# Linear attention's output gates as four pairs of half-size products

## The chip, the cores and the metric

One core of one Trainium2 chip. The metric is the device time of one execution in microseconds (us), the median of several. On the core, TensorE (PE) multiplies, ScalarE (ACT) and VectorE (DVE) do the elementwise work, GpSimd (POOL) and SyncE (SP) mostly start DMA transfers. Each works through its own list of instructions, and semaphores tie the lists together.

## The reference, cut to what matters

The program is a decoder of two layers over 528 tokens (16 of them meta tokens) with a width of 1024. Each layer has two feed-forward networks (FFNs) around a mixer. The mixer of the first layer is the gated linear attention (GLA) that the change is about:

```
q, k, v, r, lr = split(hn @ w_in)            # 512, 512, 1024, 1024, 16 columns
gk = log_sigmoid(lr @ w_gate + b_gate) / 16
... per head (4) and chunk (64): o = causal(q_dec k_dec^T) v + q_dec state
o = rmsnorm(o, g_head) * silu(r)             # r: the output gates
return o @ w_out
```

The gates are r = hn @ w_r, 1024 x 1024 over 528 tokens: eight tiles of 128 rows of r each.

## The kernel before, in words

Everything is computed in fp32 accuracy from pairs of an upper and a lower part: a value w becomes w0 = round(w) (an ACT copy to fp32r) and w1 = w - w0 (a DVE subtraction), and a product is the sum of three matmuls, w0 x0, w1 x0 and w0 x1. `mm3` and its relatives record them all at L202.

TensorE's order is written out by the Python code itself. Generators ("jobs") yield estimated times to a virtual clock (`Flow`, L76 on); whatever records matmuls advances the clock by their cost, and a job goes on when the clock has come to it. ACT's, DVE's and POOL's lists are then made from that recording by the scheduler, so the yields (STEP, STATE_KEYS 1.5, SCALED 2.2, BEHIND 2.2) decide how much other work stands between two steps of a job, not how long anything waits on the chip. Weights come in units. `load_unit` issues a unit's DMAs on SP into "raw" slots (13 of 128 x 512), `split_unit` makes the two parts of a plain unit (ACT L271, DVE L274), `set_ahead` says how far loading runs ahead. A unit that is a list of two tiles is made by `split_pair` into the seven factors 11, s1, s2, 12, s3, s4, 22 of a Strassen product (ACT L291, DVE L292): the sums s1 to s4 come partly from two accumulating DMAs on POOL (L350), partly from DVE additions (L297). All parts, of weights and of tokens alike, share one pool of 40 "pair" slots (128 x 2 x 528).

The FFNs' two large products run that way: `Strassen` holds the PSUM banks, an `Item` runs seven half-size products (two halves of the rows by two halves of the 528 tokens), and `right_factors` makes the seven token factors 11, t1, 22, t2, 21, t3, t4 (ACT L998, DVE L999, differences L1008) from scaled copies xs of the residual H (L1013). Since the factors need room, `right_factors` writes H to DRAM (`h_kept`), and later code brings it back.

GLA ran with plain tiles instead. In the stage (`gla`, from L1228) the first four tiles k, q, v, v of head 0 come first, then for each head h the coroutine `core(h)` runs while `x_units` multiplies the next head's four tiles. `core` holds the scans of the log gates (L1307, L1308), transposes of the values (pv), exponentials, keys' transposes (pk), scores (pa, pb), states (ps), outputs (po, pn), the reciprocal roots of the outputs' norms (`half_roots`, ten small DVE steps L477 to L486 on a tile half_go), the scaling of the outputs with them on ACT (on, L1406, and onm for the meta tokens, L1407), and transposes back (pt, PE L214). Behind head 3's tiles `x_units` multiplies the eight gate tiles, each over token groups of 272 and 256 columns, while heads 2's end and head 3 run. `gated(m, g, p)` takes one tile and group: times the token norm (L1430), tanh on ACT, the gate (L1432), times the head's output (L1437), then split into parts og (ACT L540, DVE L541). `out_proj` multiplies og by the output weights (y on PE).

## Time and profile before

| | us |
|---|---|
| median of three runs | 1844.48 (1844.38 to 1844.85) |
| the profiled execution itself | 1848.01 |
| its span, first to last instruction | 1846.2 |
| PE busy in the span | 1834.5 |
| DVE, ACT busy | 1459.9, 1119.6 |
| the GLA stage's heads and gates (405 to 557 us): DVE busy | 102.0 of 152 |
| the last 198 matmuls of the gate tiles | 533.0 to 557.2 |

How to read it: the span is that of one profiled execution, the median that of unprofiled ones; differences worked out in the span are carried over to the median. A row of a timeline is start, length, engine, line, operation, out<-in, shape, count, and in brackets how long the engine was idle before it and who ended that. Names in the profile leave out buffer numbers: x is a tile's PSUM bank, w a weight part, zl0f a token factor of layer 0's first FFN, w_s a weight sum, half_go the roots.

### The profile page before, as it was taken

To read this page: it belongs to the slowest core of one execution; us is meant where nothing else is said; L and a number is where in the kernel's file an instruction comes from. 1 tells how busy PE (TensorE), PEld (TensorE's weight loads), DVE (VectorE), ACT (ScalarE), POOL (GpSimd) and SP (SyncE) were. 2 spreads that over 40 slices of the span, in tenths; PEclk is the share of its full clock that TensorE was granted. 3 is DMA by queue.
4 is the path that set the end of the run, shared out by engine and by line. 5 is a ranking of instruction groups with operands and counts; after the bars stand their busy time and mean duration, and the time that the engine had idled before them with its cause. 6 is when DMAs were issued, how large, how long until landed. Compare 5 with 4: busy or idle time off the path is not lost.

```text
span 1846.2 us, 38789 instructions
## 1 busy us (share of the span) xinstructions
PE 1834.5 (99%) x14743; PEld 1780.8 (96%) x14743; DVE 1459.9 (79%) x3029; ACT 1119.6 (61%) x2613; POOL 324.0 (18%) x487
## 2 busy tenths in 40 slices
PE   9999999999999999999999999999999999999998
PEld 9999999999999999999999899999987898999998
DVE  6889888666664788988878789898667678898884
ACT  6666666654446566665665566666558765666564
POOL 2210101320001411011133110112320042111122
PEclk9999999999999999999999999999999999999999
DMA  6756659421213366666853565768421226657681
GB/s 244 196 152 156 166 150 247 151 70 58 69 58 115 105 173 154 155 167 151 252 180 104 143 161 148 181 151 243 153 80 47 70 91 162 161 152 175 156 252 49
DMA packets 143371, 269.98 MB, mean 146 GB/s; under 512 B 16080, under 2 KB 36432, under 8 KB 143184
## 3 DMA queue, kind: packets, MB, share of 16 engines
q1 hardware_dynamic: 113056, 194.94, 32.8%
q0 software_dynamic: 29696, 71.97, 19.6%
q8 instruction: 115, 1.88, 0.4%
q14 instruction: 72, 0.59, 0.1%
q10 hardware_dynamic: 432, 0.59, 0.1%
HBM read 230.74 MB, written 36.18 MB: 145 GB/s over the span
## 4 chain that ended last, share of the span: by engine, by line
PE 93%; DVE 4%; ACT 2%; issue 1%; DMA 1%; DVEq 0%; SPq 0%; POOLq 0%; ACTq 0%
PE a L202 28%; PE x L202 22%; PE y L202 17%; PE c L202 13%; PE d L202 7%; PE o L202 1%; DVE w L292 1%; PE po L202 1%; DVE w_s L292 1%; ACT s L1623 1%; DVE raw L297 1%; DMA raw<-in_w_in 1%; ACT w_s L291 0%; PE pt L214 0%; PE sa L202 0%
## 5 line engine op out<-in xcount | busy, mean ns | idle before, releaser
L292 DVE TENSOR_TENSOR w_s<-raw,w_s 128x512 fp32r<-128x512 f32 (+1 forms) x416 | 264.2, 646 | 73.6 <-ACT w_s L291 69.6
L291 ACT ACTIVATE w_s<-raw 128x512 fp32r<-128x512 f32 (+1 forms) x416 | 241.0, 592 | 89.2 <-DVE raw L324 49.2
L292 DVE TENSOR_TENSOR w<-raw,w 128x512 fp32r<-128x512 f32 (+1 forms) x312 | 196.2, 645 | 4.0
L274 DVE TENSOR_TENSOR w<-raw,w 128x512 fp32r<-128x512 f32 x248 | 164.5, 695 | 37.0 <-ACT w L271 34.7
L350 POOL DMA_DIRECT2D raw<-in_w_in x112 | 103.4, 967 | 453.2 <-DVE w L292 97.1
L291 ACT ACTIVATE w<-raw 128x512 fp32r<-128x512 f32 (+1 forms) x312 | 177.7, 589 | 0.0
L297 DVE TENSOR_TENSOR raw<-raw,raw 128x512 f32<-128x512 f32 (+1 forms) x256 | 162.7, 636 | 2.2
L202 PE MATMUL x<-x_l0m,w 128*128 128x272 f32 (+1 forms) x1152 | 152.2, 289 | 0.0
L202 PEld LDWEIGHTS x<-x_l0m,w 128*128 128x128 f32 x1152 | 143.4, 188 | 2.7 <-issue 1.7
L271 ACT ACTIVATE w<-raw 128x512 fp32r<-128x512 f32 x248 | 144.1, 620 | 2.5 <-DMA raw<-in_w_in 1.2
L535 POOL TENSOR_TENSOR acc_post<-acc_post,sq_post 128x256 f32<-128x256 f32 (+1 forms) x77 | 61.7, 802 | 360.8 <-ACT sq_post L534 357.2
L202 PE MATMUL y<-hidl0f,w 128*128 128x272 f32 (+1 forms) x960 | 119.3, 285 | 0.0
L202 PEld LDWEIGHTS y<-hidl0f,w 128*128 128x128 f32 x960 | 117.9, 188 | 0.2
L202 PE MATMUL a<-zl0f_t,w_s 128*128 128x264 f32 x864 | 116.8, 284 | 0.0
L202 PE MATMUL y<-hidl1f,w 128*128 128x256 f32 (+1 forms) x768 | 114.8, 310 | 0.0
L202 PE MATMUL a<-zl1f_t,w_s 128*128 128x256 f32 x864 | 113.8, 281 | 0.0
L202 PEld LDWEIGHTS y<-hidl1f,w 128*128 128x128 f32 x768 | 104.9, 188 | 8.5
L202 PEld LDWEIGHTS a<-zl0f_t,w_s 128*128 128x128 f32 x864 | 109.9, 188 | 0.0
L202 PEld LDWEIGHTS a<-zl1f_t,w_s 128*128 128x128 f32 x864 | 107.1, 188 | 0.0
L1213 POOL DMA_DIRECT2D kept_y<-dn x32 | 36.3, 1134 | 400.5 <-DVE w_s L292 203.7
L202 PE MATMUL x<-x_l0f,w 128*128 128x256 f32 (+1 forms) x768 | 98.9, 289 | 1.5 <-ACT w L271 1.1
L202 PEld LDWEIGHTS x<-x_l0f,w 128*128 128x128 f32 x768 | 96.2, 191 | 2.2 <-ACT w L271 1.3
(568 smaller groups left out, 4118.7 us busy)
## 6 DMA issues: line engine op xcount, KB each, us to landing
raw<-in_w_in SPq DMA_DIRECT2D x408, 256.0 KB, 4.2
raw<-in_w_in POOLq DMA_DIRECT2D x112, 256.0 KB, 5.4
raw<-in_w_down SPq DMA_DIRECT2D x128, 192.0 KB, 2.4
raw<-in_w_last SPq DMA_DIRECT2D x48, 256.0 KB, 4.9
raw<-in_gla_in SPq DMA_DIRECT2D x48, 256.0 KB, 3.2
kept_y<-dn POOLq DMA_DIRECT2D x16, 528.0 KB, 8.2
raw<-in_w_out SPq DMA_DIRECT2D x32, 256.0 KB, 3.1
kept_y<-dn POOLq DMA_DIRECT2D x16, 512.0 KB, 8.6
```

The source lines that it names most:

```text
L202: inst = pe.matmul(o, lhs, rhs, start=start, stop=stop, skip_group_check=onto)
L271: high = act.activation(w[:, 0, :m], raw[:, :m], AF.Copy)
L274: dve.tensor_tensor(w[:, 1, :m], raw[:, :m], w[:, 0, :m].bitcast(F32), op=ALU.subtract)
L291: act.activation(w[:, 0, :m], src, AF.Copy)
L292: dve.tensor_tensor(w[:, 1, :m], src, w[:, 0, :m].bitcast(F32), op=ALU.subtract)
L297: return dve.tensor_tensor(dst, dst, src, op=ALU.add)
L350: added = pool.dma_start(r, src, accum_op=ALU.add)
L535: pool.tensor_tensor(sums[0][:, :n], sums[0][:, :n], t[:, :n], op=ALU.add)
L1213: pool.dma_start(y_sum[:, 2 * self.q : 2 * self.q + 2, o : o + 2 * n], self.y[:, :, : 2 * n], accum_op=ALU.add)
L1623: act.activation(s[:, c], s[:, c], AF.Exp, scale=rc[:, c % 2 : c % 2 + 1], bias=nm[:, c : c + 1], accum_out=den[:, c : c + 1],)
```

## The change

The sixteen plain units of the heads stay; the eight gate tiles become four paired units 64 to 67 (`GLA_PAIRS`). When the code comes to head 1, a job makes the token factors (`right_factors` for GLA's own normed input, with its differences' and parts' pace at 1.2 instead of STEP 1.1). Three of its four scratch tiles come from another pool ("dn"), so H goes out to DRAM here too and its four loads back (`bring_back_h`) stand on POOL behind the gates. The first paired unit waits in `plain` until the first parts are made. A new `Projected` runs the seven products of a pair and puts the two tiles of gates together from them; one c bank instead of two. Gating then works on one tile of 528 columns at a time. Loading ahead is set to 16 with a ring instead of 8. The heads 1 to 3 yield BESIDE = 3.0 more before the keys' transposes and 1.5 more before the transposes back; head 0 has the room that it had.

```diff
-GLA_ORDER = [4, 0, 8, 9, 5, 1, 10, 11, 6, 2, 12, 13, 7, 3, 14, 15] + list(range(16, 24))
+GLA_ORDER = [4, 0, 8, 9, 5, 1, 10, 11, 6, 2, 12, 13, 7, 3, 14, 15]
+GLA_PAIRS = [(16, 17), (18, 19), (20, 21), (22, 23)]
...
+                units += [[a["gla_in"][u] for u in pair] for pair in GLA_PAIRS]
...
-        xs = [pair_tile(f"xs{x.name}_{k}", F32) for k in range(0, KD, 2)]
+        xs = [yp.tile([P, 2, TOK], F32, tag="dn", name=f"xs{x.name}_{k}") for k in range(0, KD - 2, 2)]
+        xs.append(pair_tile(f"xs{x.name}_{KD - 2}", F32))
...
+    class Projected(Item):
+        nk = 4
...
+        def body(self):
+            self.product(self.c, "s1", "t1", True)
+            act.activation(self.second[1], self.c, AF.Copy, scale=self.scale)
+            self.product(self.a, "s2", "t2", False)
+            act.activation(self.first[1], self.a, AF.Copy)
+            self.product(self.d, "12", "21", False)
+            act.activation(self.first[0], self.d, AF.Copy)
+            self.product(self.a, "s3", "t3", False)
+            dve.scalar_tensor_tensor(self.second[1], self.a, self.scale, self.second[1], op0=ALU.mult, op1=ALU.add)
+
+        def tail(self):
+            self.product(self.c, "s4", "22", False)
+            dve.tensor_tensor(self.first[1], self.c, self.first[1], op=ALU.add)
+            self.product(self.a, "22", "t4", False)
+            act.activation(self.second[0], self.a, AF.Copy, scale=self.scale)
...
-                yield STATE_KEYS + (0 if h else BEHIND)
+                yield STATE_KEYS + (BESIDE if h else BEHIND)
...
-                yield SCALED
+                yield SCALED + (BESIDE / 2 if h else 0)
...
-            def gated(m, g, p):
+            def gated(m):
+                gs, th = rg[m]
                 act.activation(th, gs, AF.Tanh, scale=0.5)
+                yield 0.8
                 dve.scalar_tensor_tensor(gs, th, 1.0, gs, op0=ALU.add, op1=ALU.mult)
+                yield cores[m // 2]
+                yield 0.8 + m % 2 * 1.5
...
+                if h == 1:
+                    flow.spawn(right_factors(x, halves, z, plain, 1.2))
...
-            set_ahead(8)
-            x_units(x, KD, L0, lambda i, g, p: jobs.append(flow.spawn(gated(i, g, p))))
-            flow.wait(*jobs[:12])
+            plain.finish(flow)
+            set_ahead(16, RING)
+            tiles = Strassen(z, halves, 1)
...
+            bring_back_h(slice(0, TOK))
+            flow.wait(*jobs[:6])
```

How instructions move is shown at three places; numbers in names are buffer numbers.

First, the last six of the ten reciprocal-root steps of head 2 on DVE (half_go2), before the change, with what followed them (V1_3 are value rows of head 3, b3 its scans):

```order
L481 TENSOR_SCALAR half_go2_6431<-half_go2_6431 128x5
L482 TENSOR_TENSOR half_go2_6431<-half_go2_6431 128x5
L483 SCALAR_TENSOR_TENSOR half_go2_6431<-half_go2_6431 128x5
L484 TENSOR_TENSOR half_go2_6431<-half_go2_6431 128x5
L485 SCALAR_TENSOR_TENSOR half_go2_6431<-half_go2_6431 128x5
L486 SCALAR_TENSOR_TENSOR half_go2_6431<-half_go2_6431 128x5
L1256 TENSOR_TENSOR V1_3_6479<-x63_0_6387,R_l0m_5018 128x272
L1256 TENSOR_TENSOR V1_3_6479<-x63_1_6388,R_l0m_5018 128x256
L274 TENSOR_TENSOR w67_0_6534<-raw67_0_6475,w67_0_6534 128x512
L274 TENSOR_TENSOR w67_1_6537<-raw67_512_6477,w67_1_6537 128x512
L1307 SCALAR_TENSOR_TENSOR b3_6570<-resets_4978,ls23_5498 128x528
L1308 SCALAR_TENSOR_TENSOR b3_6570<-resets_4978,ls23_5498 128x528
```

After the change DVE has there (zl0m_t30 is a token factor, w64 are factors of the first pair):

```order
L1293 TENSOR_TENSOR V1_3_6500<-x63_1_6389,R_l0m_5018 128x256
L480 TENSOR_SCALAR half_go2_6508<-sums2_6463 128x5
L295 TENSOR_TENSOR w64_11_6546<-raw64_0_6488,w64_11_6546 128x512
L481 TENSOR_SCALAR half_go2_6508<-half_go2_6508 128x5
L1006 SCALAR_TENSOR_TENSOR zl0m_t30_6596<-xsl0m_0_5735,zl0m_t30_6596 128x528
L482 TENSOR_TENSOR half_go2_6508<-half_go2_6508 128x5
L1344 SCALAR_TENSOR_TENSOR b3_6599<-resets_4978,ls23_5498 128x528
L483 TENSOR_TENSOR half_go2_6508<-half_go2_6508 128x5
L1345 SCALAR_TENSOR_TENSOR b3_6599<-resets_4978,ls23_5498 128x528
L484 TENSOR_SCALAR half_go2_6508<-half_go2_6508 128x5
L300 TENSOR_TENSOR raw64_0_6488<-raw64_0_6488,raw64_3_6491 128x512
L485 TENSOR_TENSOR half_go2_6508<-half_go2_6508 128x5
```

What stood behind the roots now stands between their steps, along with parts of the pair and of the tokens. ACT's list behind the scaling of head 2's outputs is, after the change:

```order
L1444 ACTIVATE onm2_6462<-pn2_6460,half_go2_6508 16x256
L1352 ACTIVATE vt3_6602<-pv3_0_6603 128x4x128
L1005 ACTIVATE zl0m_t31_6624<-xsl0m_2_5736 128x528
L294 ACTIVATE w65_11_6647<-raw65_0_6581 128x512
L1125 ACTIVATE d64_6577<-a64_0_6574 128x264
L1352 ACTIVATE vt3_6602<-pv3_1_6618 128x4x128
L1453 ACTIVATE V1_2_6074<-pt2_0_6628 128x512
L1005 ACTIVATE zl0m_t40_6650<-xsl0m_4_5737 128x528
L1453 ACTIVATE V1_2_6074<-pt2_1_6640 128x512
L1361 ACTIVATE d3_6653<-b3_6599 128x528
L1363 ACTIVATE d3_6653<-b3_6599 128x528
L294 ACTIVATE w64_s1_6660<-raw64_3_6491 128x512
```

The upper part of s1 of pair 64 has become the eleventh instruction behind onm2.

Second, PE's list between head 2's transposes back (pt2) and those of head 3's values (pv3), before the change (x64 is the last tile of head 3, x65 the first gate tile):

```order
L214 MATMUL pt2_1_6527<-ident_78,on2_6404 128x128 x4
L1415 MATMUL pm2_t_6513<-ident_78,onm2_6405 128x16
L202 MATMUL x64_0_6482<-x_l0m_5_4924,w63_1_6127 128x272 x3
L202 MATMUL x64_1_6483<-x_l0m_5_4924,w63_1_6127 128x256 x3
L202 MATMUL x64_0_6482<-x_l0m_6_4951,w63_1_6127 128x272 x3
L202 MATMUL x64_1_6483<-x_l0m_6_4951,w63_1_6127 128x256 x3
L202 MATMUL x64_0_6482<-x_l0m_7_5000,w63_1_6127 128x272 x3
L202 MATMUL x64_1_6483<-x_l0m_7_5000,w63_1_6127 128x256 x3
L202 MATMUL x65_0_6565<-x_l0m_0_4802,w64_0_6240 128x272 x3
L214 MATMUL pv3_0_6574<-ident_78,V1_3_6479 128x128 x4
L202 MATMUL x65_1_6566<-x_l0m_0_4802,w64_0_6240 128x256 x3
L202 MATMUL x65_0_6565<-x_l0m_1_4828,w64_0_6240 128x272 x3
```

and the same place after it, where 57 matmuls of the tiles x63 and x64 stand between pn2 and the first row:

```order
L204 MATMUL d64_6577<-zeros_81 128x264
L204 MATMUL a64_0_6574<-zl0m_110_5883,w64_11_6546 128x264 x3
L216 MATMUL pv3_0_6603<-ident_78,V1_3_6500 128x128 x4
L204 MATMUL a64_0_6574<-zl0m_110_5883,w64_11_6546 128x264 x3
L204 MATMUL a64_0_6574<-zl0m_111_5922,w64_11_6546 128x264 x6
L216 MATMUL pv3_1_6618<-ident_78,V1_3_6500 128x128 x4
L216 MATMUL pt2_0_6628<-ident_78,on2_6461 128x128 x4
L1452 MATMUL pm2_t_6627<-ident_78,onm2_6462 128x16
L216 MATMUL pm3_6636<-ident_78,V1_3_6500 16x128 x2
L216 MATMUL pt2_1_6640<-ident_78,on2_6461 128x128 x4
L1452 MATMUL pm2_t_6627<-ident_78,onm2_6462 128x16
L204 MATMUL c64_0_6576<-zl0m_t10_5994,w64_s1_6660 128x264 x6
```

All tiles of head 3 now stand ahead of pt2, and in place of the gate tile x65 stand the first two products of pair 64, one per factor.

Third, DVE's list ahead of the last two tiles of the gated output, og6 and og7, before the change:

```order
L1437 SCALAR_TENSOR_TENSOR rg7_7276<-rg7_7276,vec_77,V1_3_6479 128x272
L1437 SCALAR_TENSOR_TENSOR rg7_7276<-rg7_7276,vec_77,V1_3_6479 128x256
L541 TENSOR_TENSOR og7_7283<-rg7_7276,og7_7283 128x272
L274 TENSOR_TENSOR w75_0_7324<-raw75_0_7252,w75_0_7324 128x512
L541 TENSOR_TENSOR og7_7283<-rg7_7276,og7_7283 128x256
```

and after it (w72 to w75 are weights of the output projection):

```order
L1466 SCALAR_TENSOR_TENSOR rg6_7128<-rg6_7128 128x528
L1471 SCALAR_TENSOR_TENSOR rg6_7128<-rg6_7128,vec_77,V1_3_6500 128x528
L1466 SCALAR_TENSOR_TENSOR rg7_7129<-rg7_7129 128x528
L1471 SCALAR_TENSOR_TENSOR rg7_7129<-rg7_7129,vec_77,V1_3_6500 128x528
L277 TENSOR_TENSOR w72_1_7334<-raw72_512_7193,w72_1_7334 128x512
L277 TENSOR_TENSOR w73_0_7337<-raw73_0_7241,w73_0_7337 128x512
L277 TENSOR_TENSOR w73_1_7340<-raw73_512_7243,w73_1_7340 128x512
L277 TENSOR_TENSOR w74_0_7356<-raw74_0_7281,w74_0_7356 128x512
L277 TENSOR_TENSOR w74_1_7359<-raw74_512_7283,w74_1_7359 128x512
L544 TENSOR_TENSOR og6_7372<-rg6_7128,og6_7372 128x528
L544 TENSOR_TENSOR og7_7391<-rg7_7129,og7_7391 128x528
```

Five weight parts moved in front of the lower parts of og6 and og7.

More of the change, by code (lines that the diff above doesn't have):

```diff
@@ L974, in ffn, with bring_back_h @@
                     pool.dma_start(Y[:, 2 * q : 2 * q + 2, kept], y_sum[:, 2 * q : 2 * q + 2, kept])
+        bring_back_h(kept)
+        set_ahead(32)
+        cap[0] = min(end, len(units))
+        for _ in proj:
+            pass
+    def bring_back_h(kept):
         H.fresh()
@@ L978, in ffn, with right_factors @@
             pool.dma_start(H[:, rows, kept], h_kept[:, rows, kept])
-        set_ahead(32)
-        cap[0] = min(end, len(units))
-        for _ in proj:
-            pass
-    def right_factors(x, halves, z, plain):
+    def right_factors(x, halves, z, plain, step=STEP):
         for job in x.rjob:
@@ L1179, in tail, with __init__, right @@
             return job if self.step is None else None
+    class Projected(Item):
+        nk = 4
+        def __init__(self, tiles, first, second, scale=1.0):
+            super().__init__(tiles)
+            o, n = tiles.o, self.n
+            self.first, self.second = ([t[:, c : c + n] for c in (o, o + n)] for t in (first, second))
+            self.scale = -scale
+        def right(self, name, k):
+            flow.until(lambda: len(self.tiles.z.get(name, ())) == 2)
+            return (self.tiles.z[name][k // 2][:, i, k % 2] for i in range(2))
+        def body(self):
[12 more added lines that the diff above has]
+            act.activation(self.second[0], self.a, AF.Copy, scale=self.scale)
+            released[0] += 1
     class Down(Item):
@@ L1449, in gla, with gating, finish_gates, begin @@
                     late = x_units(x, 4, L0, lambda i, g, p, kk=kk: evac(*kk[i], g, p))
+            plain.finish(flow)
+            set_ahead(16, RING)
+            tiles = Strassen(z, halves, 1)
             jobs = []
-            set_ahead(8)
-            x_units(x, KD, L0, lambda i, g, p: jobs.append(flow.spawn(gated(i, g, p))))
-            flow.wait(*jobs[:12])
+            def gating(m):
+                rg[m], rg[m + 1] = duo(f"rg{m}"), duo(f"rg{m + 1}")
+                return Projected(tiles, rg[m][0], rg[m + 1][0])
+            def finish_gates(m):
+                jobs.extend([flow.spawn(gated(m)), flow.spawn(gated(m + 1))])
+            plan = [(lambda m=m: gating(m), lambda m=m: finish_gates(m)) for m in range(0, KD, 2)]
+            def begin(i):
+                if i == len(plan):
+                    return None
+                t = plan[i][0]()
+                t.head()
+                return t
+            cur = begin(0)
+            for i in range(len(plan)):
+                cur.body()
+                nxt = begin(i + 1)
+                cur.tail()
+                plan[i][1]()
+                cur = nxt
+            bring_back_h(slice(0, TOK))
+            flow.wait(*jobs[:6])
             set_ahead(16)
```

27 lines of the change are left out of this document (12 added, 15 removed).

## The prediction

> **What bounds the kernel now.** I read the page first: the busy times, the chain that ended last, the costliest groups. Here are its lines on the engines, the chain by engine, and the two groups that make the parts of a paired weight (columns: line, engine, operation, out<-in, count; busy us, mean ns; idle before).
>
> ```profile
> PE 1834.5 (99%) x14743; PEld 1780.8 (96%) x14743; DVE 1459.9 (79%) x3029; ACT 1119.6 (61%) x2613; POOL 324.0 (18%) x487
> PE 93%; DVE 4%; ACT 2%; issue 1%; DMA 1%; DVEq 0%; SPq 0%; POOLq 0%; ACTq 0%
> L292 DVE TENSOR_TENSOR w_s<-raw,w_s 128x512 fp32r<-128x512 f32 (+1 forms) x416 | 264.2, 646 | 73.6 <-ACT w_s L291 69.6
> L291 ACT ACTIVATE w_s<-raw 128x512 fp32r<-128x512 f32 (+1 forms) x416 | 241.0, 592 | 89.2 <-DVE raw L324 49.2
> ```
>
> TensorE (PE) works 99% of the span and 93% of the chain. A microsecond of matmuls less is a microsecond won, as long as nobody else comes late. Who could come late is a question of stages, so next I read the stretches of the gated attention stage, and for comparison one stretch of an FFN, which already runs such products (columns: window, length, then busy us and count of PE, PEld, DVE, ACT, POOL; granted clock, DMA share, GB/s).
>
> ```profile
> 405.00:430.00 25.00, 25.00 (x202) 24.36 (x202) 19.49 (x39) 16.73 (x28) 0.00 (x0) 1.00 0.26 85
> 430.00:455.00 25.00, 25.00 (x184) 22.89 (x183) 16.79 (x43) 10.89 (x30) 0.10 (x1) 1.00 0.15 43
> 455.00:480.00 25.00, 25.00 (x191) 23.17 (x190) 15.17 (x38) 11.96 (x32) 0.10 (x1) 1.00 0.20 64
> 480.00:503.00 23.00, 23.00 (x166) 21.28 (x166) 12.58 (x32) 9.47 (x27) 0.00 (x0) 1.00 0.14 46
> 503.00:530.00 27.00, 27.00 (x205) 25.40 (x203) 18.72 (x52) 12.47 (x37) 0.00 (x0) 1.00 0.12 40
> 530.00:557.00 27.00, 27.00 (x221) 26.61 (x221) 19.23 (x44) 11.71 (x27) 0.00 (x0) 1.00 0.28 89
> 160.00:200.00 40.00, 40.00 (x330) 39.99 (x329) 34.88 (x67) 24.53 (x57) 6.99 (x8) 1.00 0.85 196
> ```
>
> PE does not stall anywhere in the stage. DVE works 101.98 of its 152 us (the six rows added) and so idles 50 us. In the FFN stretch DVE works 87% and PE still does not stall.
>
> **The gain.** Two rows of PE's timeline give the price of a matmul (start, length, count): the last gate tiles in one run, and the output projection behind them.
>
> ```profile
> 533.00 24.32 PE L202 MATMUL x<-x_l0m,w 128*128 128x272 f32 x198
> 557.16 36.68 PE L202 MATMUL y<-og,w 128*128 128x272 f32 x297
> ```
>
> From 533.00 to 557.16 stand 198 matmuls, so 122.0 ns each. Before, the gates take 8 tiles x 8 blocks of d x 2 token groups x 3 = 384 matmuls. After, they take 4 pairs x 7 products x 4 blocks x 3 = 336, of 264 columns, which is what the two groups before (272 and 256) have on average, so I keep the price. 384 x 0.1220 = 46.8 us, 336 x 0.1220 = 41.0 us, and one zero matmul costs 0.1: the gain is **5.8 us**, if PE never waits.
>
> **The added work.** The factors of the tokens need 8 scaled copies, 8 differences and 14 parts, each part one copy on ACT and one subtraction on DVE. The FFN's rows price them (ns: least, median, most); a difference is counted like a part's subtraction, which has its width and engine:
>
> ```profile
> L1013 DVE SCALAR_TENSOR_TENSOR xsl0f<-H,vec,R_l0f x16: 757/759/765, 40.3 to 650.8; 128x528 f32<-128x528 f32 x16
> L999 DVE SCALAR_TENSOR_TENSOR zl0f_t<-xsl0f,zl0f_t x16: 691/700/708, 59.8 to 679.5; 128x528 fp32r<-128x528 f32 x16
> L998 ACT ACTIVATE zl0f_t<-xsl0f x16: 628/636/647, 58.9 to 678.4; 128x528 fp32r<-128x528 f32 x16
> ```
>
> DVE: 8 x 0.759 + 22 x 0.700 = 21.5 us; ACT: 14 x 0.636 = 8.9 us. The weights: 4 pairs make 28 parts and 8 sums where 8 tiles made 16 parts, so DVE gets 12 parts and 8 sums at about 0.646, 12.9 us more, and ACT 12 x 0.592 = 7.1 us. The gating gives some back:
>
> ```profile
> L1437 DVE SCALAR_TENSOR_TENSOR rg<-rg,vec,V 128x272 f32<-128x272 f32 x8 | 4.0, 497 | 0.0
> ```
>
> Before, a tile has four kinds of such instructions on two groups, of which this is the dearest: 8 x 8 x about 0.45 (an estimate under its 0.497) = 29 us. After, three kinds on 528 columns (at 0.70 to 0.76, by the rows of that width above) and 8 half-width evacuations make some 21 us (24 x 0.72 + 8 x 0.45), with the rest of the evacuation on ACT (about 4 us). Together DVE gets about 26 us more and ACT about 20. Against DVE's 50 idle us this fits **on the average**, and its price is nothing wherever the queues run ahead of PE. It costs where PE waits for one particular instruction. In the trace's rows each engine works its list in order, so for three such instructions I count what now stands in front.
>
> **First place: head 0's transposes.** The extra room before the transposes is given only to heads 1 to 3. In the trace:
>
> ```profile
> 437.85 0.17 DVE L477 TENSOR_SCALAR half_go<-sums 128x5 f32<-128x5 f32 x1 [2.85 <-ACT onm L1399]
> 441.05 0.16 DVE L486 SCALAR_TENSOR_TENSOR half_go<-half_go 128x5 f32<-128x5 f32 x1
> 441.38 1.56 ACT L1406 ACTIVATE on<-po,half_go 128x256 f32<-128x256 f32 x4
> 442.80 0.45 ACT L1407 ACTIVATE onm<-pn,half_go 16x256 f32<-16x256 f32 x1
> 444.06 0.60 PE L214 MATMUL pt<-ident,on 128*128 128x128 f32 x4
> ```
>
> Before, the square roots take from 437.85 to 441.2, the normalised rows are there at 443.25, and PE comes for them at 444.06: 0.8 us of slack. Now two differences and a part of the tokens (3 x about 0.62 at the pace of a full queue), a copy, two products and half a scaling (0.3 + 2 x 0.6 + 0.35) stand between the ten small steps, and 0.5 us less of other work: some 3.2 us more, of which I count 2.4, since the first of them can fill DVE's 2.85 idle us. PE waits **1.6 us**. Bounds: 0 (all of it fits into that idle time) and 2.4 (none does).
>
> **Second place: the first product that uses the sum s1 of pair 64.** The same chain of head 2 (pn is PE's last matmul of the head before the roots):
>
> ```profile
> 487.07 0.60 PE L202 MATMUL pn<-vm,am 128*16 128x256 f32 x2
> 487.61 7.58 PE L202 MATMUL x<-x_l0m,w 128*128 128x272 f32 x60
> 495.02 0.60 PE L214 MATMUL pt<-ident,on 128*128 128x128 f32 x4
> ...
> 488.55 0.17 DVE L477 TENSOR_SCALAR half_go<-sums 128x5 f32<-128x5 f32 x1 [0.35 <-ACT onm L1399]
> 490.36 0.17 DVE L486 SCALAR_TENSOR_TENSOR half_go<-half_go 128x5 f32<-128x5 f32 x1
> 494.27 1.25 DVE L1307 TENSOR_TENSOR_SCAN b<-resets,ls 128x528 f32<-128x528 f32 x1
> 495.44 1.23 DVE L1308 TENSOR_TENSOR_SCAN b<-resets,ls 128x528 f32<-128x528 f32 x1
> ...
> 490.61 1.57 ACT L1406 ACTIVATE on<-po,half_go 128x256 f32<-128x256 f32 x4 [2.17 <-DVE half_go L486]
> 492.41 1.14 ACT L271 ACTIVATE w<-raw 128x512 fp32r<-128x512 f32 x2
> ```
>
> I count from the start of pn2. PE after the change: pn2 0.54, then 57 matmuls x 0.1235 = 7.0, the zero matmul and 12 products 1.6, four groups of four transposes 2.2, three small ones 0.5: it wants s1 at 11.8 us. DVE: the value rows wait for nine of the 57 matmuls and end at about 2.4. Then come ten root steps of 0.2 with a weight part, a token part, both scans of head 3 (1.17 apart) and a weight sum among them: 2.0 + 0.6 + 0.6 + 2.3 + 0.6 = 6.1, so the roots are there at 8.5, not at 3.5 as now. ACT starts 0.25 later, scales for 1.8 (490.61 to 492.41) until 10.5, and has then ten instructions of about 0.53 and a narrow one of 0.3 up to and with the upper part of s1, so 16.1; the lower part on DVE follows 0.6 later, 16.8 - 11.8 = **5.0 us** of waiting. Bounds: 2.2 if ACT's list is no hindrance and only DVE's own list counts (from the roots at 8.5 another nine instructions of about 0.6), and 6.5 if three of the handovers between ACT and DVE cost a step of 0.5 each. Behind it stand the next parts of the same pair at one part per 0.6 to 0.7 us on each engine, while PE needs 1.47 us per product: I add **1.1 us** for two products that find their part late (bounds 0 and 2.5).
>
> **Third place: the start of the output projection.** Its first products use tiles 0 to 5 of the gated output: 54 matmuls x 0.122 = 6.6 us of cover. Then it needs the lower parts of tiles 6 and 7. After the last gate product these take an ACT copy, a tanh, two wide instructions per tile on DVE (2.7), five weight parts that now stand ahead (5 x 0.61 = 3.1) and one subtraction: 0.7 + 0.6 + 2.7 + 3.1 + 0.6 = 7.7. PE waits **1.1 us**. Bounds: 0, and 5 by the third rival.
>
> The stored residual costs four DMAs out and, on POOL's queue, four back behind the last gate factors. Nothing waits for the four out. POOL has no other work there (0.00 busy in the last two gate stretches), so I take the four back at nothing themselves; their cover is the projection's 36 us, and what they collide with is the third rival.
>
> **Sum.** -5.8 + 1.6 + 5.0 + 1.1 + 1.1 = **+3.0 us**. The profiled execution took 1848.01 us, its span 1846.2; the sum is a difference within it (1848.01 to 1851.0), and against the median of 1844.48 it gives **1847.5 us**. With the waits at their lower bounds the sum is -3.6, at their upper ones (5 in the third place) +10.6; since they share their causes but not their places, I take 1844 to 1850.5 for this case alone. A measurement of this kernel can tell about 0.2%, 3.7 us, from no change: faster is below 1840.8, slower above 1848.2.
>
> **Rivals.** (1) *The queues keep pace.* The FFN stretch speaks for it: DVE is busier there (87%) than it would be here (128 of 152 us, 84%), and PE never waits. Against it: no heads' chains with scans and roots run in that stretch. Then only the gain is left, 1844.48 - 5.8 = 1838.7. That the change does not do what it says is no rival: 336 matmuls stand in the new list.
>
> (2) *The long wait cools TensorE.* The windows of the opening are the only ones that I found with a lower grant:
>
> ```profile
> 5.00:10.00 5.00, 3.54 (x21) 3.13 (x20) 3.44 (x8) 3.55 (x8) 0.00 (x0) 0.84 1.02 362
> 10.00:15.00 5.00, 5.00 (x35) 5.00 (x34) 3.95 (x8) 3.86 (x10) 0.00 (x0) 0.82 1.08 362
> ```
>
> PE idled 1.46 us in the first of them and the grant stayed low through the second, in which PE was always busy. The loss is (0.16 + 0.18) x 5 = 1.7 us. If the 5 us wait does that once, the time is 1847.5 + 1.7 = 1849.2. In the windows shown of the stage the grant is 1.00 and PE has no such gap, so the trace neither bears it out nor excludes it. [...]
>
> (3) *The residual's way back makes the output weights late.* This ends slower. In the FFN before, the same four loads went beside weight loads (group rows of the DMA issues: the first two from 318 to 332 us, the last from 540 to 560; KB each, median us to landing):
>
> ```profile
> raw<-in_gla_in SPq DMA_DIRECT2D x11, 256.0 KB, 8.6
> H<-kept_h POOLq DMA_DIRECT2D x4, 528.0 KB, 7.1
> ...
> raw<-in_gla_out SPq DMA_DIRECT2D x3, 256.0 KB, 2.6
> ```
>
> Beside the residual a weight block landed 8.6 us after its issue; the output weights now take 2.6. So a block issued in the same moments can be 6 us late, and DVE's list has weights 72 to 74 ahead of gated tiles 6 and 7. It decides from the point at which block 74 lands later than about 4 us after the last gate product, when DVE comes to it; then the third place grows from 1.1 to about 5, and the time is 1851.4. Against it: those blocks are asked for in part before the residual.
>
> **How the numbers follow.** The forecast gets 0.52, the queues that keep pace 0.18, the cooled clock 0.12, the late weights 0.18. The likeliest gives 1847.5. The range of 8 in 10 goes from 1840.0, which takes in the faster rival with 1.3 us of waiting, to 1852.0, which takes in the third rival. Faster: 0.18, rival 1 nearly whole and a shred of the forecast. Slower: rivals 2 and 3, and 0.14 of the forecast, whose upper third lies above 1848.2: 0.44. The rest, 0.38, is the same.
>
> **What would show it.** The gain: 336 matmuls of 264 columns at 122 ns. The first place: a PE gap before head 0's pt, ended by ACT's on. The second: one PE gap of 4 to 6 us before the c product of the first pair, ended by DVE's w_s1. The third: about 1 us before the y matmuls that use the last two tiles, ended by DVE's og. Rival 1 would show none of the three; rival 2 a window under 1.00 right behind the second place; rival 3 weights that land 6 us and more after their issue, and DVE idle ahead of og. I am wrong most likely in the second place: if ACT's and DVE's lists start earlier than I count them, since all their work before pn2 may be done sooner or later than in the trace of before.

## The result, and the profile after

The changed kernel took **1853.37 us** (median of six runs, 1852.34 to 1854.19) beside 1844.61 us of the kernel before: a ratio of 1.0041, 95% interval 1.0031 to 1.0052. Measured again beside the kernel before (e9 below) it was 1852.58 against 1846.45, ratio 1.0033 (1.0021 to 1.0046). So it is slower by 6 to 9 us, 0.3 to 0.5%. I had forecast 1847.5 in a range of 1840.0 to 1852.0: the time lies above it.

These are the stage's stretches after the change (window, length, busy us and count of PE, PEld, DVE, ACT, POOL; granted clock, DMA share, GB/s):

```profile
480.00:503.00 23.00, 23.00 (x172) 21.23 (x172) 10.97 (x30) 6.58 (x22) 0.00 (x0) 1.00 0.00 1
503.00:530.00 27.00, 23.12 (x158) 21.71 (x157) 24.14 (x47) 17.41 (x37) 1.74 (x2) 0.87 0.43 110
530.00:557.00 27.00, 25.53 (x195) 23.98 (x194) 22.33 (x47) 21.24 (x52) 2.17 (x4) 1.00 0.44 140
557.00:580.00 23.00, 22.75 (x185) 22.68 (x186) 16.60 (x26) 18.30 (x41) 2.56 (x3) 1.00 0.76 265
```

PE, full before, now misses 3.9 us in one stretch and 1.5 in the next, and in the first of them the grant (the share of TensorE's full clock that it is given) is 0.87. PE's list of waits names the places, and its timeline gives their sizes:

```profile
PE c L204 <- ACT w_s L294: 3.4, 1, 3.4
PE a L204 <- ACT rg L1205: 1.7, 1, 1.7
PE pt L216 <- ACT on L1443: 0.4, 1, 0.4
PE c L204 <- DVE w_s L295: 0.3, 1, 0.3
```

```profile
364.89 1.28 PE L204 MATMUL x<-x_l0m,w 128*128 128x272 f32 x9
...
444.79 1.43 PE L216 MATMUL pt<-ident,on 128*128 128x128 f32 x4 [0.39 <-ACT on L1443]
...
491.92 0.60 PE L204 MATMUL pn<-vm,am 128*16 128x256 f32 x2
...
503.39 0.23 PE L1452 MATMUL pm_t<-ident,onm 16*128 16x16 f32 x1
507.05 0.59 PE L204 MATMUL c<-zl0m_t,w_s 128*128 128x264 f32 x1 [3.43 <-ACT w_s L294]
507.96 2.79 PE L204 MATMUL c<-zl0m_t,w_s 128*128 128x264 f32 x11 [0.33 <-DVE w_s L295]
510.55 2.57 PE L204 MATMUL a<-zl0m_t,w_s 128*128 128x264 f32 x12
512.95 1.64 PE L204 MATMUL d<-zl0m,w 128*128 128x264 f32 x12
...
553.89 1.64 PE L204 MATMUL d<-zl0m,w 128*128 128x264 f32 x12
557.25 1.74 PE L204 MATMUL a<-zl0m_t,w_s 128*128 128x264 f32 x12 [1.73 <-ACT rg L1205]
...
561.74 1.55 PE L204 MATMUL y<-og,w 128*128 128x272 f32 x11
```

From pn2 at 491.92 to the first product with s1 at 507.05 pass 15.1 us, to its second matmul 16.0. After that, 23 matmuls take 4.99 us (507.96 to 512.95), 217 ns each instead of 122, at a grant of 0.50 in the window from 508 to 511 us: that is the low grant, and it makes them 2.2 us longer.

The measure that carries the rest is the **stretch** of the stage, from its first matmul (x<-x_l0m) to the first of the output projection (y<-og). Before it was 557.16 - 364.70 = 192.46 us, after it is 561.74 - 364.89 = 196.85: **4.39 us longer**. Added up by starts in the trace, the 384 plain gate matmuls took 47.7 us, and the 336 matmuls of the products with their zero matmul take 47.3. Of these, 5.2 are waits and the low grant, so without them they would take 42.1. The rest of the 4.39 us is head 0's transposes (+0.9), the heads' x matmuls (+0.2), the wait behind 503.39 (+3.5) and 0.2 in the other transposes.

The spans of the two profiled executions differ by 5.1 us (1846.2 and 1851.3), the first medians by 8.8. The granted clock falls once more near 1401 us (0.61 and 0.71 in the windows from 1400 to 1410 us before, 0.69 and 0.62 from 1405 to 1415 after). By the times and mean clocks of the single runs (e1 below) it does so in some runs of either kernel, which costs 0, about 1.5 or about 3 us, and the runs of before in the first comparison had this less often than those beside e1 and e9.

### The profile page after: what moved, and what is told of

It is laid out like the page before. It is cut to its first block, busy times and chain, and to the rows that moved or that the text cites. A ratio compares the mean times of both kernels' runs of the same rounds, so it can differ in the third digit from the quotient of the medians.

```text
span 1851.3 us, 38794 instructions
## 1 busy us (share of the span) xinstructions
PE 1833.2 (99%) x14696; PEld 1777.2 (96%) x14696; DVE 1481.9 (80%) x3047; ACT 1139.4 (62%) x2643; POOL 333.8 (18%) x499
## 4 chain that ended last, share of the span: by engine, by line
PE 90%; DVE 5%; ACT 3%; DMA 1%; issue 1%; SPq 0%; DVEq 0%; ACTq 0%
PE a L204 29%; PE x L204 17%; PE y L204 17%; PE c L204 14%; PE d L204 7%; PE o L204 1%; ACT s L1688 1%; PE po L204 1%; DVE w L295 1%; DVE w_s L295 1%; DMA H<-in_h 1%; DVE raw L300 1%; DMA raw<-in_w_in 0%; ACT w_s L294 0%; PE pt L216 0%
## 5 line engine op out<-in xcount | busy, mean ns | idle before, releaser
L295 DVE TENSOR_TENSOR w_s<-raw,w_s 128x512 fp32r<-128x512 f32 (+1 forms) x432 | 274.8, 647 | 77.8 <-ACT w_s L294 73.8
L294 ACT ACTIVATE w_s<-raw 128x512 fp32r<-128x512 f32 (+1 forms) x432 | 250.8, 593 | 89.0 <-DVE raw L327 49.3
L295 DVE TENSOR_TENSOR w<-raw,w 128x512 fp32r<-128x512 f32 (+1 forms) x324 | 204.3, 646 | 5.5 <-ACT w L294 1.4
L294 ACT ACTIVATE w<-raw 128x512 fp32r<-128x512 f32 (+1 forms) x324 | 185.1, 590 | 0.0
L277 DVE TENSOR_TENSOR w<-raw,w 128x512 fp32r<-128x512 f32 x232 | 153.8, 695 | 27.6 <-ACT w L274 26.2
L300 DVE TENSOR_TENSOR raw<-raw,raw 128x512 f32<-128x512 f32 (+1 forms) x264 | 168.0, 636 | 2.3
L274 ACT ACTIVATE w<-raw 128x512 fp32r<-128x512 f32 x232 | 134.8, 620 | 1.8 <-PE y L204 1.1
L204 PE MATMUL x<-x_l0m,w 128*128 128x256 f32 (+1 forms) x768 | 102.2, 289 | 0.0
L204 PEld LDWEIGHTS x<-x_l0m,w 128*128 128x128 f32 x768 | 95.8, 188 | 1.6 <-issue 0.8
```

Of the source, the lines that this page charges most:

```text
L204: inst = pe.matmul(o, lhs, rhs, start=start, stop=stop, skip_group_check=onto)
L274: high = act.activation(w[:, 0, :m], raw[:, :m], AF.Copy)
L277: dve.tensor_tensor(w[:, 1, :m], raw[:, :m], w[:, 0, :m].bitcast(F32), op=ALU.subtract)
L294: act.activation(w[:, 0, :m], src, AF.Copy)
L295: dve.tensor_tensor(w[:, 1, :m], src, w[:, 0, :m].bitcast(F32), op=ALU.subtract)
L300: return dve.tensor_tensor(dst, dst, src, op=ALU.add)
```

## The experiments

All times are medians, the kernel before is measured side by side with each group of experiments; the ratio is that of the single runs and can differ a little from the quotient of the medians. The stretch is from the profiled execution, by the two starts named above.

| | us | before | ratio (95%) | stretch |
|---|---|---|---|---|
| e1 before, unchanged | 1846.27 | 1847.31 | 0.9997 (0.9988 to 1.0006) | 192.48 |
| e2 before, later by 36 matmuls | 1852.23 | 1847.31 | 1.0024 (1.0015 to 1.0034) | - |
| e3 wait filled | 1852.79 | 1847.31 | 1.0032 (1.0021 to 1.0043) | 196.66 |
| e4 more room for head 3 | 1848.02 | 1847.31 | 1.0000 (0.9991 to 1.0009) | 192.15 |
| e5 later split | 1852.48 | 1846.48 | 1.0036 (1.0024 to 1.0049) | 195.41 |
| e6 e4 and two c banks | 1847.96 | 1846.48 | 1.0009 (1.0000 to 1.0018) | 193.51 |
| e7 all four | 1844.41 | 1846.48 | 0.9986 (0.9977 to 0.9995) | 187.41 |
| e8 fill at 1401 us | 1847.94 | 1846.48 | 1.0008 (1.0000 to 1.0017) | 192.48 |
| e9 after, unchanged | 1852.58 | 1846.45 | 1.0033 (1.0021 to 1.0046) | 197.12 |
| e10 e7, weights held | 1842.19 | 1846.45 | 0.9981 (0.9972 to 0.9989) | 187.40 |
| e11 factors alone | 1846.71 | 1846.45 | 1.0004 (0.9996 to 1.0013) | 193.80 |
| e12 half of e4 | 1850.44 | 1846.45 | 1.0023 (1.0013 to 1.0034) | 194.00 |

The medians hold more or fewer runs with the later fall of the clock. The profiled executions can be compared ahead of it: the first matmul of the second layer's scores (sa<-kz,q) starts at 1367.20 us before, at 1372.64 after (+5.4), in e9 at +5.9, in e1 at -0.1, in e4 at +0.8, in e11 at +1.8, in e7 at -1.8 and in e10 at -4.2.

**e1, e2 and e9: how much of the 8.8 us is the change?** e1 is the kernel before as it is, e9 the changed one as it is. e2 adds idle matmuls to the kernel before:

```diff
             flow.wait(*jobs[:12])
+            spare, q = ps("spare")[:, :264], 66
...
+            for _ in range(36):
+                mm(spare.rearrange("p (a c) -> p a c", c=q), zeros, zeros[:, :q].unsqueeze(1).to_broadcast([P, 4, q]))
...
             set_ahead(16)
```

> The kernel before, unchanged, to see its single executions with their clocks. Theory A (a second clock drop): in the two profiles the grant falls to half for 6.8 us at 1401 us (before) and at 1407 us (after), far behind the change; a run of before without that drop takes 1844.4, one with it 3.4 to 3.8 us more, about 1848. I expect the executions at 1844.4 with a mean clock one step higher than those at 1848, and most of them at 1844.4. Rival B (the 3.5 us between the profiled execution of before and its median are the profiler's): the profiled execution at about 1848, all others at 1844.4, and the clock the same in all.

> The kernel before with 36 idle matmuls (zeros on a spare bank) between the gates and the output projection: PE gets 36 x 0.122 = 4.4 us later everywhere behind, nothing else changes. Theory A with a phase that is fixed to the program's start: the gaps of the shared-attention stage at 1401 us fall otherwise into the clock's windows, the drop comes in nearly every run as in the changed kernel, 1844.5 + 4.4 + 3.5 = 1852.4. Theory A with a phase that is free from run to run: 1848.9 in most runs and 1852.4 in some, no more often than in the kernel before. Rival B (no such drop outside profiles): 1848.9 in all.

> The changed kernel, unchanged, beside the kernel before in one call. Theory A (the drop at 1401 to 1407 us comes or not by a phase that is free in each run, in both kernels alike): the kernel before spreads over 1844.2 to 1848.5, its median near 1846.5 to 1847.3, and the changed one over 1849 to 1854, so that the ratio is 1.0030 to 1.0036, not 1.0041. Rival (the changed kernel always hits the later drop): all of it at 1852 to 1854 again, ratio 1.0036 or more.

The 28 runs of the kernel before that stand beside e1 to e4 lie in three groups, and their mean clocks go with them: seven near 1844.7 (clocks 0.999 and 1.000), five near 1846.1 (0.999), and sixteen from 1847.2 to 1848.8 (0.998, mean 1847.8). Here are windows at the same place of the profile before, and of e7, whose execution had no fall there:

```profile
1395.00:1400.00 5.00, 4.25 (x50) 3.46 (x50) 5.00 (x15) 5.00 (x17) 0.00 (x0) 1.00 0.15 33
1400.00:1405.00 5.00, 3.73 (x19) 2.57 (x20) 4.43 (x13) 3.21 (x11) 0.00 (x0) 0.61 0.55 158
1405.00:1410.00 5.00, 5.00 (x37) 4.28 (x33) 3.29 (x9) 3.49 (x13) 0.00 (x0) 0.71 0.20 75
```

```profile
1395.00:1400.00 5.00, 3.00 (x28) 2.27 (x27) 5.00 (x14) 5.00 (x17) 0.00 (x0) 1.00 0.22 49
1400.00:1405.00 5.00, 5.00 (x47) 4.07 (x46) 4.93 (x18) 4.37 (x16) 0.00 (x0) 1.00 0.67 216
```

The trace's record of the grant before has it at half for 3.413 us from 8.41 us and for 6.827 us, twice as long, from 1401.05, and the groups are about 1.5 us apart: I read them as runs with no such piece of 3.413 us near 1401 us, with one and with two. So theory A holds, except that most runs were not at 1844.4: that was the rarer case. The profiled execution of before (1848.01, mean clock 0.997) was one with two pieces, that of e1 (1846.39, 0.999) one with one. The place was not the same in the two: the falls begin at 1401.05 us in the one and at 1403.04 in the other, by the trace's record, for the same kernel. e2 agrees: shifted by 4.4 us, the kernel shows three runs at 1849.3 to 1849.9 (clocks 0.999 and 1.000) and seven at 1852.2 to 1853.0 (0.998), and against all runs of before the ratio gives 0.0024 x 1847 = 4.4 us, no more than the matmuls. e9 spreads from 1850.5 to 1854.8, and its ratio fell to 1.0033. The change itself costs 5 to 6 us; nearly 3 of the first 8.8 were the luck of the runs.

**e3: what does the low grant at 506 us cost?** Ahead of the first product with s1:

```diff
         def body(self):
+            if self.tiles.count == 1:
...
+                for _ in range(28):
+                    mm(self.c.rearrange("p (a c) -> p a c", c=q), zeros, zeros[:, :q].unsqueeze(1).to_broadcast([P, 4, q]))
...
             self.product(self.c, "s1", "t1", True)
```

> The changed kernel with 28 idle matmuls (zeros on the bank c that is about to be overwritten) ahead of the first product with s1 of pair 64, where PE waits 3.4 us: PE is busy there instead of waiting, and does nothing earlier. Theory C (the wait makes the granted clock fall, and that costs some 2.2 us behind it, 23 matmuls in 4.99 us instead of 2.82): no grant below 1 between 500 and 520 us, the stage ends 2 us earlier, 1851.2 or less. Rival (the slow matmuls behind the wait are late weights, not clock): nothing gained, 1853.4, or 0.2 lost.

PE's timeline in e3:

```profile
504.39 3.81 PE L204 MATMUL c<-zeros 128*128 128x264 f32 x28
508.04 0.28 PE L204 MATMUL c<-zl0m_t,w_s 128*128 128x264 f32 x1
508.80 1.62 PE L204 MATMUL c<-zl0m_t,w_s 128*128 128x264 f32 x11 [0.48 <-DVE w_s L295]
511.42 0.39 PE L204 MATMUL a<-zl0m_t,w_s 128*128 128x264 f32 x1 [1.00 <-ACT w_s L294]
512.14 1.60 PE L204 MATMUL a<-zl0m_t,w_s 128*128 128x264 f32 x11 [0.34 <-DVE w_s L295]
```

Behind the fill no low grant shows: its 28 matmuls took 3.65 us and the last 11 above 1.44, so 130 and 131 ns each, where the changed kernel's 23 took 217. But the stretch gained 0.19 us only: PE now waits for s2. In ACT's list of e3 the emptying of bank c has come to stand ahead of s2's upper part, which begins at 510.74 in e3 and at 507.44 in the changed kernel. So the low grant went with the wait (without that wait, no fall there), but its price at this place, 2.2 us if the parts had been ready, was not measured: the fill moved a list too. In e5 the fall was one piece instead of two; there the third product began 0.66 us earlier behind the first than in the changed kernel, but the fifth only 0.35, since other parts were late. The price stays open between about 0.35 and 2.2.

**e4 and e12: is the second place the main loss?** e4 has both lines, e12 only the first:

```diff
             def core(h, before):
...
+                if h == HEADS - 1:
+                    yield 6.0
...
-                yield SCALED + (BESIDE / 2 if h else 0)
+                yield SCALED + (BESIDE / 2 if h else 0) + (3.0 if h == HEADS - 2 else 0)
```

> The changed kernel with head 3's scans and exponentials begun 6 later on the virtual clock, and head 2's transposes back 3 later, so that on DVE and ACT the sum s1 of pair 64 no longer stands behind them. Theory D (the second place of the prediction is the main loss: 4.6 us of waiting and the clock drop of 2.2 us that it brings): PE waits at most 1 to 1.5 us there, no drop at 505 us; the stage ends 5 to 6 us earlier, 1847 to 1848.5, and 3.5 less where the drop at 1401 us goes too. Rival E (ACT and DVE have no room for the added work in this stage, so a wait that is taken away returns at another place): head 3's transposes or the pairs 65 to 67 wait instead, and the time stays within 2 us of 1853.4.

> The changed kernel with head 3's scans begun 6 later, without the later transposes of head 2 (one of the two parts of e4_room). Theory D by the count of the lists: s1 is there in time, but the roots still stand between eight long instructions, so the transposes back come at 11.7 us after pn2 where PE is at 9.2: one wait of about 2.4 us at pt2 in place of 3.5 and 0.9 at s1; stretch about 193.5. Rival (the scans alone were the trouble): no wait over 0.5 us there, stretch 192 or less.

PE's waits in e4, then in e12:

```profile
PE c L204 <- DVE rg L1213: 1.4, 1, 1.4
PE a L204 <- ACT rg L1205: 1.3, 2, 1.0
PE pt L216 <- ACT on L1445: 0.4, 1, 0.4
```

```profile
PE a L204 <- ACT rg L1205: 3.3, 1, 3.3
PE a L204 <- DVE w_s L295: 0.9, 1, 0.9
PE pt L216 <- ACT on L1445: 0.4, 1, 0.4
```

In both the wait for s1 is gone, and with it the fall at 506 us (the grant is 1.00 over e4's 405 to 557 us; in e12 the 24 matmuls from 503.55 to 506.57 took 126 ns each); e4 is 4.7 us shorter in the stretch, and its runs are level with the kernel before. Theory D holds for the main loss. But rival E was half right: new waits came, in e4 1.4 and 1.3 us for PSUM banks that had not been emptied, in e12 3.3 us of that kind. My count for e12 (2.4 us at pt2) was wrong: there pt lost 0.7 us more than in the changed kernel, and the larger wait came 20 us later, where I had not counted:

```profile
524.37 0.63 PE L204 MATMUL a<-zl0m_t,w_s 128*128 128x264 f32 x3 [3.26 <-ACT rg L1205]
```

This wait is about as long as the one at 507 us after the change, and no fall shows behind it: the nine matmuls from 525.20 took 1.17 us, 130 ns each.

**e5 and e6: a bank that is emptied late.** e5 is the changed kernel with a yield ahead of a split, e6 is e4 with a second bank:

```diff
                 dve.scalar_tensor_tensor(gs, gs, gn, V[:, m], op0=ALU.mult, op1=ALU.mult)
+                yield 2.0
                 split(og[m], gs, (0, TOK))
```

```diff
-            tiles = Strassen(z, halves, 1)
+            tiles = Strassen(z, halves)
```

> The changed kernel with one yield of 2.0 between a gated tile's last product with V and its split, so that on ACT the evacuation of bank a of pair 67 (line 1205 of the changed kernel) stands ahead of the split of og4, which waits for DVE. Theory F (PE's 1.9 us wait at 557 us is ACT standing idle on that split, 2.2 us by its timeline, with the evacuation behind it): that wait goes, the stretch from the first matmul of the stage to the first of the output projection falls from 196.85 to about 195.0. Rival (the prediction's third place: DVE is simply late there with the weights of the output projection, and og6 and og7 come no earlier): the wait moves to the start of y and the stretch up to the last y matmul stays as it is.

> The kernel with more room for head 3 (e4_room) with two c banks instead of one. In its trace PE waits 1.4 us before pair 65's first product for the DVE addition that empties the one c bank. Theory G (the single bank is a cost of the change, about 1.4 us): the stretch of the stage falls from 192.15 to about 190.7. Rival E (DVE is behind anyway): PE waits for a late part instead, 192 and more.

In the changed kernel ACT does nothing for 2.2 us ahead of the wait at 557 us, because og's split stands first and waits for DVE, with the emptying of bank a right behind it:

```profile
553.43 0.63 ACT L294 ACTIVATE w<-raw 128x512 fp32r<-128x512 f32 x1
556.28 0.64 ACT L543 ACTIVATE og<-rg 128x528 fp32r<-128x528 f32 x1 [2.22 <-DVE rg L1471]
556.83 0.37 ACT L1205 ACTIVATE rg<-a 128x264 f32<-128x264 f32 x1
```

In e5 that wait is gone (stretch -1.4, of which 0.7 is the shorter fall at 508 us in this execution), and PE waits as long later, in the projection, for og; here are PE's rows and, behind the dots, DVE's:

```profile
560.64 7.11 PE L204 MATMUL y<-og,w 128*128 128x272 f32 x56
569.37 2.83 PE L204 MATMUL y<-og,w 128*128 128x272 f32 x19 [1.62 <-DVE og L544]
...
564.41 4.29 DVE L277 TENSOR_TENSOR w<-raw,w 128x512 fp32r<-128x512 f32 x7
568.62 1.31 DVE L544 TENSOR_TENSOR og<-rg,og 128x528 fp32r<-128x528 f32 x2
```

Seven weight parts in one unbroken row stand ahead of the two og, so it is DVE's list that is late and not their loads. So both readings were right: the place of the wait was ACT's list (theory F), its cause was DVE's (the rival, which is the prediction's third place), and undoing one alone brought nothing. e6 went the same way: the wait for bank c is gone, and the next bank is late instead, with a fall of the grant at 523.6 us behind it (mean clock of that execution 0.999, of e4's 1.000). Theory G fell.

```profile
PE a L204 <- ACT rg L1205: 2.7, 2, 2.5
```

**e7 and e10: all repairs together.** e7 has the lines of e4, e5 and e6, and BESIDE / 2 for head 0 as well. e10 holds the loading of output weights at the fourth until the gated tiles are recorded:

```diff
+            cap[0] = used[0] + 8
             cur = begin(0)
...
-            flow.wait(*jobs[:6])
+            flow.wait(*jobs)
```

> Head 3's room, the later split, two c banks and the extra room before head 0's transposes together. If the waits are separate (D, F, G and the prediction's first place) the stretch falls from 192.15 by 1.4 (bank), 1.3 (evacuation behind splits), 0.5 (head 0) to about 189, that is 3.5 below the kernel before, and the runs come at 1841 without the drop at 1401 us, 1844.5 with it. By rival E (no room on ACT and DVE) it stays at 191 to 192.5.

> The kernel with all four repairs (e7_all) and the loading of output weights held at the fourth until the last two gated tiles are recorded, so that on DVE no weight 72 to 75 stands ahead of og6 and og7. In e7_all PE waits 1.6 us at 561 us for og. The prediction's third place (those weights in DVE's list are the cause): the wait goes, time 1.6 below e7_all, 1841.3 in runs without the late drop, 1842.8 as a median. Rival (the third rival of the prediction: the residual's four loads now go ahead of weights 72 to 75): PE waits for a weight some 23 us into the projection instead, nothing gained or 2 lost.

e7's stretch fell further than I had counted (187.41, not 189), but 2.0 us of that are lost again in the projection. One wait is left, the third place, and in e10 not even that:

```profile
PE y L204 <- DVE og L544: 1.5, 1, 1.5
```

```profile
503.00:530.00 27.00, 26.93 (x204) 25.52 (x204) 24.73 (x49) 18.57 (x41) 1.71 (x2) 1.00 0.45 128
530.00:557.00 27.00, 27.00 (x214) 25.86 (x214) 24.35 (x50) 22.12 (x52) 2.17 (x4) 1.00 0.70 237
...
405.00:557.00 152.00, 151.93 (x1153) 143.24 (x1153) 126.08 (x271) 94.41 (x217) 9.33 (x14) 1.00 0.36 102
```

The last row is e10's whole stage: DVE works 126.08 of 152 us, 24 more than before, and PE waits 0.07. Rival E falls with it: there is room for all of the added work, given its order. The late weights of e10's own rival did not come either: in the projection and behind it, up to 900 us, PE waits for nothing. e10 is **faster than the kernel before**, ratio 0.9981 (0.9972 to 0.9989), 3.5 us, and 10.4 us faster than the changed kernel beside it (e9). Its stretch is 5.06 us below before: 42.9 us for the products against 47.7 for the plain tiles is 4.8 of it.

**e8: keeping PE busy at 1401 us.** Ten idle matmuls ahead of the transposes there, in the kernel before:

```diff
                 pm = ps(f"ptm{u}_{hf}")
+                if i == 4:
...
+                    for _ in range(10):
+                        mm(pm[:, :256].rearrange("p (a c) -> p a c", c=64), zeros, zeros[:, :64].unsqueeze(1).to_broadcast([P, 4, 64]))
...
```

> The kernel before with ten idle matmuls (zeros, 256 columns, into the bank that the transposes then overwrite) ahead of the transposes at 1401 us, where PE waits 1.26 us for ACT. Theory A (PE idles 2.3 of 3.4 us there, in some runs within one window of the clock, and only then the grant falls to half): no drop in any run, all at 1844.4 to 1845.2, some 2 us below the mean of the kernel before in the same call. Rival (the drop has another cause, or ten matmuls are too few or themselves make the transposes late): the three groups at about 1844.6, 1846.1 and 1847.7 stay, or all lie 0.3 to 1 higher.

```profile
1400.96 2.50 PE L202 MATMUL ptm<-zeros 128*128 128x256 f32 x10 [1.26 <-ACT pm L1654]
```

This tests nothing: what PE waits for there is that very bank, so the fill waited too and then made the transposes 2.3 us late. Whether the grant would stay at 1.00 at 1401 us with the gap filled was not shown, and that idling counts by windows of 3.4 us there was an assumption of mine: the traces' records show the lengths and the spacing of the falls.

**e11: the added work without the products.** Rooms, factors, the residual out and back, on the kernel before; the diff is the change's own lines for these, and the factors are used by nobody.

> The kernel before, gates as plain tiles, with only the token factors made beside heads 1 and 2 and used by nobody, the residual out and back, and the changed rooms. Theory D (what costs is one product's part standing behind head 3's scans in the lists, not the amount of work): DVE has 21.5 us more and PE waits only in the prediction's first place, 1.0 to 1.5 us; the stretch is 193.5 to 194.0. Rival E (the amount of work on DVE and ACT is too much for the stage): waits of 3 us and more at heads 2 and 3, 195.5 or more.

```profile
PE pt L215 <- ACT on L1411: 0.4, 1, 0.4
```

One wait, in the prediction's first place, stretch 193.80, +1.34. DVE is busy 16.6 us longer in the span (the forecast 21.5 adds up lengths that overlap: in the changed kernel a part's subtraction of 0.70 us begins at 507.82 and the next instruction at 508.44). The factors' work alone does no harm at heads 2 and 3; the pairs' weights are not in this kernel. Its median is level with before by luck: nine of its eleven runs lie at 1846.3 to 1846.9, by their clocks (0.999 and 1.000) without the later fall, where the kernel before without it takes 1844.3 to 1845.2 (0.999 and 1.000).

## Why the prediction was wrong, point by point

- **The gain.** 5.8 us forecast, 5.6 measured in the changed kernel (47.7 - 42.1) and 4.8 in e10 (47.7 - 42.9), where PE hardly waits. The price of 122 ns is the median of both kinds of matmul; with what stands between them the plain tiles took 124 ns apiece, the products 125 and, in e10, 127. Right.
- **First place.** 1.6 us forecast. Against the kernel before, head 0's transposes pt cost 0.9 and the heads' x matmuls 0.2: 1.1 us. With room for head 0 (e7 against e6) 0.90 and 0.55 come back. Right in its mechanism and a little too dear.
- **Second place.** I had counted 16.8 us from pn2 to the product; the trace has 15.1 to its first and 16.0 to its second matmul. PE's own work took 11.6, not 11.8. 4.3 us against 5.0 forecast, with the root steps ending at 499.63, 7.7 after pn2 (I had 8.5). Right in its mechanism: e4 took it away. The 1.1 us added for the products behind it was 0.3 as a wait. Together I had put 1.5 us too much here.
- **Third place.** 1.1 us at the start of y. It came to 1.9 us, one pair earlier, at a bank that ACT emptied late, for the reason that the prediction gave (weights ahead of the gating on DVE); e5 moved it to where I had put it, e10 removed it. The size was too small by almost half, and the place was one list further on than I had followed.
- **The step that failed** is the sum's basis and the term that the sum put at nothing, the low grant of the second rival. Of the 5.9 us between forecast and median, 3.5 are the basis: I added the sum up within a profiled execution of 1848.01 us and set it against a median of 1844.48, and said only how the two stood to each other. I wrote that the opening's windows were the only ones found with a lower grant. In the same trace the grant was 0.61 and 0.71 from 1400 to 1410 us: (0.39 + 0.29) x 5 = 3.4 us, so that fall is nearly all of the 3.5 us. The three runs behind the median were all without it, which was luck; by their times and clocks (0.996 and 0.997) nearly all of the six runs after had it. The other 2.4 us lie within the profiled executions, 1851.0 forecast and 1853.38 measured. They are mainly the low grant behind the long wait, 2.2 us, to which I gave a chance of 0.12 and nothing in the sum, when the profile had an example at 1401 us: a fall after gaps of 0.74 and 1.26 us. With a wait of 3.4 us the fall came in all three profiles of the changed order (after, e5, e9; mean clocks 0.996, 0.998, 0.996), 1 or 2 pieces of 3.413 us long; behind e12's wait of 3.3 us the matmuls took 130 ns each. The price of 1.7 us that I took from the opening does not hold there: the executions without that fall reach the stage at 364.3 to 365.7 us, the one with it at 364.70. In hindsight the rival belonged in the likeliest case, and the range needed some 3 us more at its end for the fall at 1401.
- **The third rival** did not happen: the residual's loads took 8.5 us, but the output weights beside them landed 3.4 us after their issue (median), not some 8.6, and neither PE nor DVE waited for weights 72 to 75 (DVE's seven parts in e5 follow without a pause).

The sum of the stretch as measured: -5.6 + 1.1 + 4.3 + 0.3 + 1.9 + 2.2 (the low grant, by 23 matmuls) = 4.2 of the 4.39 us; the other 0.2 is in the transposes of values. Without the low grant the terms give 2.0, against the forecast 3.0: the errors of the three places partly cancel. From the projection on, the changed kernel loses 0.7 us more by 820 us, where the list of PE's waits shows nothing; what it loses it by stays open.

## What to carry to other kernels

Work that fits on the average (DVE 126 of 152 us) can still cost what it saves: count, for each product that PE will want, what stands ahead of its last part in the lists of the engines that make it, and follow that into the emptying of the banks, because a wait that is taken away alone came back one list further on (e5, e6, e12). All repairs together turned 6 us of loss into 3.5 us of gain. And before a sum is made against a profiled execution, its whole span should be searched for windows with a low grant: the profiled execution and the median differed here by just that, 3.5 us.

## What the runs showed of the hardware that was not expected

After the change the trace's record of the grant has it at half twice (the last 1.5 us of the span apart), from 505.81 and from 1406.93 us, for 6.827 us each time. Before, it is at half from 8.41 us for 3.413 us and from 1401.05 us for 6.827. In each of the two executions the falls begin a whole number of pieces of 3.413 us apart: 264 after, 408 before. Where these steps meet the program differed between executions (1401.05 and 1403.04 us in two of the kernel before). In the profiles before and after, the 3.413 us ahead of a fall had PE idle for 2.1 to 2.5 us (2.5 at 502.4 to 505.8 us and 2.3 at 1403.5 to 1406.9 after the change, 2.1 at 5.0 to 8.4 and 2.2 at 1397.6 to 1401.1 before), if each matmul counts for 135 ns from its start. The length of a wait did not settle it: e12's of 3.26 us had matmuls of 130 ns behind it, the changed kernel's of 3.43 us a grant of 0.50. Here are the windows of the first fall after the change:

```profile
505.00:508.00 3.00, 0.63 (x2) 0.33 (x2) 2.70 (x5) 3.00 (x7) 0.00 (x0) 0.64 0.00 0
508.00:511.00 3.00, 3.00 (x14) 3.00 (x15) 2.28 (x5) 0.80 (x3) 0.00 (x0) 0.50 0.27 87
511.00:514.00 3.00, 3.00 (x20) 3.00 (x20) 2.11 (x4) 1.97 (x6) 0.00 (x0) 0.73 0.02 5
```

From 508 us on the grant stays at half while PE works without a pause, and it comes back at 512.6 in the middle of that work. Before, the idling around the fall at 1401.05 us is two waits, of 0.74 and 1.26 us (up to 1398.84 and 1401.35), and small gaps; in e7 PE was idle for 2.00 us from 1395 to 1400, and the grant stayed at 1.00 up to 1410. So the kernel before had three times, near 1844.7, 1846.1 and 1847.8 (the 28 runs beside e1 to e4), and its median depends on their mixture.
